# Making the chunk operators of an RWKV-7 recurrence for eight chunks at once

## The chip, the cores and the metric

The kernel runs on one core of one Trainium2 chip. The metric is the device time of one execution in microseconds (us). A difference of less than 0.3% is not told from no change.

## What is computed

One layer of a streaming encoder: 1024 prompt rows and 64 sample rows of width 1024 are normalised, multiplied by one input projection of 8320 columns, and split into differential attention (8 heads) and an RWKV-7 time mixing (16 heads of 64). Both results are gated and go through one output projection. The change touches the time mixing, whose definition is a scan over rows, for each head:

```python
def step(s, inp):                      # s: 64 x 64 state of a head
    r_t, w_t, k_t, v_t, a_t, b_t = inp
    sa = jnp.einsum('bhij,bhj->bhi', s, a_t)
    s = s * w_t[:, :, None, :] + sa[..., None] * b_t[:, :, None, :] + v_t[..., None] * k_t[:, :, None, :]
    return s, jnp.einsum('bhij,bhj->bhi', s, r_t)
```

The kernel does not walk row by row. It takes chunks of 64 rows. Within a chunk the rows' effects on each other form a 64 x 64 triangular system, which is inverted; between chunks only the state is carried.

## The kernel before

**Units.** The work of the time mixing is cut into 17 units: 8 pairs of heads, two halves of 512 rows each (8 chunks of 64), and one unit for the sample rows, in which each of the 8 "chunks" is one pair of heads. A tile holds head 0 of the pair in partitions 0 to 63 and head 1 in 64 to 127.

**Stages of a unit** (function `unit`, one generator for each unit):
- preparation (L536 to L677): up-projection of decay and learning rate with weights that `load_up` fetches (L514), cumulative decay, and the tiles `pt` (decayed rows) and `bk` (undecayed keys);
- products within the chunk (`m_s`, L689 and L690: 64 contraction rows, one head in each half of the array), masked by VectorE (L702) into `lt`, `pt` and `rbk`;
- the inverse of the triangular system (L719 to L829): five levels, each of two groups of small products, three VectorE operations between them, and one refinement; its result is `xtf`;
- transposes of `bk` and of the values, copied by ScalarE into `bkt` and `suv` (L789 to L815), once the unit before has left its chain;
- the chain over the 8 chunks (L860 to L913). `suv[:, c]` holds the state that chunk c starts from, beside the chunk's values. Each chunk takes three links: product `g` (L862), copied by VectorE (L876); product with the inverse (L879), copied back by VectorE into `suv` (L885, L886); product with `bkt` (L890), from which VectorE makes the next chunk's state (L900) with the decayed old state `sd` that ScalarE made (L869, L870). Two more products for each chunk give its outputs (L867 or L882, and L891);
- group norm, gate and store.

**What sets the order.** The program is written by a planner (`Weave`): each unit is a stream that yields the time it reckons its last step to take, and a filler stream of the lowest rank takes what is left of TensorE, three matmuls of an input projection at a time (L226 to L228). After the last head's projection the filler goes on with the output projection (L1236 to L1238). `turn` lets one unit at a time into each stage, so that one unit's chain lies beside the next one's inverse and the preparation of the one after. The order is fixed when the program is built; each engine then runs its own list in order and waits where an operand is late. Once all units are stored, attention (`phase_a`) takes the place of the units, with the same filler under it.

## Time and profile before

| what | value |
|---|---|
| median of 3 runs | 1816.07 us (1812.95 to 1818.63) |
| the profiled execution's own time | 1819.35 us |
| span of the profile | 1817.6 us |
| TensorE busy | 1678.9 us, 92% |
| VectorE busy | 1248.0 us, 69% |
| ScalarE busy | 846.4 us, 47% |
| GpSimd busy | 716.0 us, 39% |
| mean granted TensorE clock | 0.98 of full speed |

The profile is one execution. PE is TensorE, DVE is VectorE, ACT is ScalarE, POOL is GpSimd, SP is SyncE, whose queue issues most transfers. A busy TensorE need not be at its peak, since ends of matmuls overlap; what one costs is read from the distance between starts.

### The profile page before, as it was taken

To read this page: it belongs to the slowest core of one execution; us is meant where nothing else is said; L and a number is where in the kernel's file an instruction comes from. 1 tells how busy PE (TensorE), PEld (TensorE's weight loads), DVE (VectorE), ACT (ScalarE), POOL (GpSimd) and SP (SyncE) were. 2 spreads that over 40 slices of the span, in tenths; PEclk is the share of its full clock that TensorE was granted. 3 is DMA by queue.
4 is the path that set the end of the run, shared out by engine and by line. 5 is a ranking of instruction groups with operands and counts; after the bars stand their busy time and mean duration, and the time that the engine had idled before them with its cause. 6 is when DMAs were issued, how large, how long until landed. Compare 5 with 4: busy or idle time off the path is not lost.

```text
span 1817.6 us, 34309 instructions
## 1 busy us (share of the span) xinstructions
PE 1678.9 (92%) x12930; PEld 1500.6 (83%) x12930; DVE 1248.0 (69%) x2606; ACT 846.4 (47%) x2027; POOL 716.0 (39%) x901
## 2 busy tenths in 40 slices
PE   7999998999989989999999889989998898988997
PEld 5988888888878988898889888989887777777875
DVE  5667777678677778778777577744566476676736
ACT  6433443434433543444354344233556675665532
POOL 3433322332322433333342333112444757666563
PEclk9999999999999999999999899999999999999999
DMA  4210222221131111111111111436546455554345
GB/s 154 65 45 27 73 71 65 59 69 29 30 103 50 37 57 33 42 46 29 45 48 43 55 56 57 125 100 178 158 110 190 123 153 167 154 142 114 94 131 165
DMA packets 204096, 158.82 MB, mean 87 GB/s; under 512 B 44085, under 2 KB 185050, under 8 KB 203930
## 3 DMA queue, kind: packets, MB, share of 16 engines
q1 hardware_dynamic: 169098, 137.33, 26.3%
q10 hardware_dynamic: 34832, 19.30, 4.1%
q8 instruction: 102, 1.67, 0.4%
q14 instruction: 64, 0.52, 0.1%
HBM read 108.67 MB, written 47.34 MB: 86 GB/s over the span
## 4 chain that ended last, share of the span: by engine, by line
PE 56%; DVE 19%; POOL 7%; DMA 6%; issue 5%; ACT 5%; ACTq 1%; SPq 1%; POOLq 0%; DVEq 0%
PE x_o L1475 2%; PE po L1236 2%; PE po L1237 2%; PE po L1238 2%; PE cbank L890 2%; PE cbank L862 2%; PE s L1414 2%; PE m_s L689 2%; PE s L1415 1%; PE pj_g L226 1%; PE cbank L879 1%; PE pj_aq L226 1%; PE pj_av L226 1%; PE pj_g L227 1%; PE pj_k L226 1%
## 5 line engine op out<-in xcount | busy, mean ns | idle before, releaser
L869 ACT ACTIVATE sd<-suv,dc 64x64 f32<-64x64 f32 x128 | 44.4, 347 | 179.0 <-DVE suv L900 150.9
L1236 PE MATMUL po<-woh,mxh 128*128 128x512 f32 x288 | 122.1, 424 | 1.5 <-DVE part L1247 0.9
L1237 PE MATMUL po<-woh,mxl 128*128 128x512 f32 x288 | 115.7, 402 | 1.5 <-POOL mxl L158 1.5
L1238 PE MATMUL po<-wol,mxh 128*128 128x512 f32 x288 | 115.3, 400 | 1.8 <-POOL wol L158 1.8
L1431 ACT ACTIVATE e<-s,nb 128x128 f32<-128x128 f32 (+7 forms) x144 | 101.1, 708 | 33.5 <-DVE nb L1424 20.4
L158 POOL TENSOR_TENSOR mxl<-mxr,mxh 128x512 fp32r<-128x512 f32 x63 | 89.0, 1414 | 55.4 <-ACT mxh L157 53.0
L1475 PE MATMUL x_o<-vn,wt 128*128 128x128 f32 (+1 forms) x608 | 87.3, 289 | 11.8 <-DVE wt L1469 3.7
L1475 PEld LDWEIGHTS x_o<-vn,wt 128*128 128x128 f32 (+1 forms) x608 | 80.5, 200 | 21.0 <-DVE wt L1465 5.1
L1424 DVE TENSOR_REDUCE nb<-s 128x1 f32<-128x640 f32 (+8 forms) x104 | 95.5, 921 | 1.9
L735 POOL TENSOR_TENSOR ltlo<-lt,lt 64x512 f16<-64x512 f32 x32 | 37.6, 1173 | 129.4 <-ACT lt L723 128.2
L1414 PE MATMUL s<-k,qs 128*128 128x512 f32 (+4 forms) x208 | 76.6, 376 | 11.3 <-ACT e L1431 9.3
L900 DVE SCALAR_TENSOR_TENSOR suv<-cbank,dc,sd 64x64 f32<-64x64 f32 x224 | 63.1, 282 | 28.6 <-PE cbank L890 23.5
L890 PE MATMUL cbank<-suv,bkt 128*128 128x128 f32 x256 | 56.3, 302 | 24.5 <-DVE suv L886 24.3
L1415 PE MATMUL s<-k,qs 128*128 128x512 f32 (+4 forms) x208 | 71.2, 360 | 3.1 <-POOL k L1344 2.1
L226 PE MATMUL pj_k<-hhi,wh_k 128*128 128x384 f32 (+1 forms) x192 | 70.1, 365 | 1.9 <-ACT raw_k L241 1.9
L226 PE MATMUL pj_aq<-hhi,wh_aq 128*128 128x384 f32 (+1 forms) x192 | 71.5, 372 | 0.0
L226 PE MATMUL pj_av<-hhi,wh_av 128*128 128x384 f32 (+1 forms) x192 | 68.8, 358 | 2.5 <-DVE fl_g L999 2.1
L890 PEld LDWEIGHTS cbank<-suv,bkt 128*128 128x128 f32 x256 | 41.2, 189 | 36.0 <-DVE suv L886 33.9
L226 PE MATMUL pj_g<-hhi,wh_g 128*128 128x384 f32 (+1 forms) x192 | 70.6, 368 | 0.0
L226 PE MATMUL pj_ak<-hhi,wh_ak 128*128 128x384 f32 (+1 forms) x192 | 70.2, 365 | 0.0
L1247 DVE TENSOR_TENSOR part<-po,part 128x512 f32<-128x512 f32 x54 | 37.0, 686 | 47.7 <-PE po L1238 47.5
L226 PE MATMUL pj_v<-hhi,wh_v 128*128 128x384 f32 (+1 forms) x192 | 69.5, 362 | 0.0
(529 smaller groups left out, 6024.9 us busy)
## 6 DMA issues: line engine op xcount, KB each, us to landing
mxr<-mixB SPq DMA_DIRECT2D x32, 256.0 KB
wor<-in_w_out SPq DMA_DIRECT2D x64, 128.0 KB
qa<-scr_q SPq DMA_DIRECT2D x32, 204.0 KB
ka<-scr_k SPq DMA_DIRECT2D x32, 204.0 KB
mxr<-mixA SPq DMA_DIRECT2D x24, 256.0 KB
scr_q<-fl_q SPq DMA_DIRECT2D x8, 544.0 KB
scr_k<-fl_k SPq DMA_DIRECT2D x8, 544.0 KB
scr_v<-fl_v SPq DMA_DIRECT2D x8, 544.0 KB
```

The costliest lines, as they stand in the source:

```text
L158: gtt(lo, raw, hi.bitcast(F32), op=SUB)
L226: mm(ps[:, :n], hi[:, k, :], hhi[i][:, k, :], start=(k == 0), stop=False)
L890: mm(s, bkt[:, c], suv[:, c], start=True, stop=True)
L900: stt(suv[r, c + 1, h, :] if c < 7 and not smp else to[r], s[r, h * CH:(h + 1) * CH], dc[r, c:c + 1], sd[r], op0=MUL, op1=ADD)
L1236: mm(ps, hi[:, q, :], wh, start=(q == 0), stop=False)
L1237: mm(ps, lo[:, q, :], wh, start=False, stop=False)
L1238: mm(ps, hi[:, q, :], wl, start=False, stop=(q == len(ks) - 1))
L1414: mm(s2[:, b:b + w], lq, k1[c][:, k0 + o_:k0 + o_ + w], start=True, stop=False)
L1415: mm(s2[:, b:b + w], lq, k2[c][:, k0 + o_:k0 + o_ + w], start=False, stop=True)
L1424: nc.vector.tensor_reduce(nb[:, 0:m], s3[:, :, 0:n], axis=AX.X, op=MAX, negate=True)
L1431: act(e[:, 0:n], s3[:, j, 0:n], AF.Exp, bias=nb[:, j:j + 1], accum_out=st["sm"][:, c:c + 1])
L1475: mm(ops[:, 0:P], wt[0:w, b, :], vn[0:w, vb, :], start=(b == 0), stop=(b == len(kbs) - 1))
```

## The change

**The operators.** For each chunk the state map is now one 128 x 128 operator. The inverse is multiplied with the transposed decayed keys (`qt`, L861 of the changed kernel), the result with the transposed `bk` and the masked output products together (`ty`, L874), and VectorE adds that to an identity and to the decayed rows in place (L879). `pt` grows from 4 to 6 columns of 64 for it: two of raw products, two of state operator, two of output operator. `xtf` needs no zeros any more and is made by one operation instead of two. The masks take strict and inclusive part in one operation (4 in place of 6 for each half).

**The chain.** A chunk takes one product (L934); ScalarE scales it by the chunk's decay straight into the next chunk's `suv` (L943). The outputs of the chunk before are one product (L919), placed one step late.

**A second stream for each unit**, `side`, of a rank just under the unit's: it transposes `bk`, the decayed keys (`ptt`) and the values while the inverse runs, and copies them by ScalarE.

**The up-projection's weights** are issued by SyncE's queue instead of ScalarE's, and the sample unit's in 8 larger transfers instead of 32.

```diff
-                    nc.scalar.dma_start(out=t[r:r + 64, s, :], in_=I[nm][0, :, q * P:(q + 1) * P])
+                    nc.sync.dma_start(out=t[r:r + 64, s, :], in_=I[nm][0, :, q * P:(q + 1) * P])
...
-            yield lambda: turn["bk"] == n and all(("r", q) in have for q in need)
+            yield lambda: turn["bk"] == n and turn["chain"] >= n - 1 and all(("r", q) in have for q in need)
...
-                vtt(pt[r, :, 2 + h, :], c3(rm)[r], dd[r, :, 1:CH + 1], op=MUL)
+                vtt(pt[r, :, 4 + h, :], c3(rm)[r], dd[r, :, 1:CH + 1], op=MUL)
+                nc.scalar.copy(pt[r, :, 2 + h, :], bch(id64)[r])
...
+                for g in range(2):
+                    ps = yield from ps512(f"at{g}{u}")
+                    for i in range(4):
+                        nc.tensor.transpose(ps[:, i * P:(i + 1) * P],
+                                            pt[:, 4 * g + i, 0:2, :].rearrange("p s t -> p (s t)"), ident)
...
+                    nc.scalar.copy(ptt[:, 4 * g:4 * g + 4, :], ps.rearrange("p (c x) -> p c x", x=P))
...
-            for h in range(2):
-                r = slice(64 * h, 64 * h + 64)
-                vtt(xtf[r, :, h, :], c3(ps)[r], c3(xt)[r], op=ADD)
+            vtt(xtf, c3(ps), c3(xt), op=ADD)
...
+                        mm(ps[r, i * P:(i + 1) * P], xtf[r, 4 * g + i, :], ptt[r, 4 * g + i, :], start=True, stop=True)
+                nc.scalar.copy(qt[:, 4 * g:4 * g + 4, :], ps.rearrange("p (c x) -> p c x", x=P))
...
+                        mm(x[:, i * P:(i + 1) * P], qt[r, c, :], wb[r, c, 1:3, :], start=True, stop=True)
...
+                    vtt(o_, x.rearrange("p (c s t) -> p c s t", s=2, t=CH), o_, op=ADD)
...
             for c in range(8):
-                mm(g, pt[:, c, 0:2, :], suv[:, c], start=True, stop=True)
-                    mm(yc, pt[:, c, 2:4, :], suv[:, c], start=True, stop=False)
-                act(sd[0:64], suv[0:64, c, 0, :], AF.Copy, scale=dc[0:64, c:c + 1])
-                act(sd[64:128], suv[64:128, c, 1, :], AF.Copy, scale=dc[64:128, c:c + 1])
-                nc.vector.tensor_copy(gsb, g)
-                mm(uu, xtf[:, c], gsb, start=True, stop=True)
-                nc.vector.tensor_copy(suv[0:64, c, 0, :], uu[0:64, 0:CH])
-                nc.vector.tensor_copy(suv[64:128, c, 1, :], uu[64:128, CH:])
-                mm(s, bkt[:, c], suv[:, c], start=True, stop=True)
-                mm(yc, rbk[:, c], suv[:, c], start=False, stop=True)
+                mm(s, pt[:, c, 2:4, :], suv[:, c], start=True, stop=True)
...
-                    stt(suv[r, c + 1, h, :] if c < 7 and not smp else to[r], s[r, h * CH:(h + 1) * CH],
-                        dc[r, c:c + 1], sd[r], op0=MUL, op1=ADD)
+                    act(suv[r, c + 1, h, :] if c < 7 and not smp else to[r], s[r, h * CH:(h + 1) * CH],
+                        AF.Copy, scale=dc[r, c:c + 1])
+                if c:
+                    outputs(c - 1)
```

Below, `cbank` is the chain's PSUM bank, `y` its outputs' bank, `pj_` a projection of the filler. TensorE, in the first chunk of a chain (pair 3, first half), before:

```order
L862 MATMUL cbank<-suv_0_6633,pt_512 128x128
L867 MATMUL y_00_6693<-suv_0_6633,pt_512 128x128
L226 MATMUL pj_g_1_6864<-hhi_170,wh_g_6528 128x384
L227 MATMUL pj_g_1_6864<-hlo_173,wh_g_6528 128x384
L228 MATMUL pj_g_1_6864<-hhi_170,wl_g_6529 128x384
L226 MATMUL pj_g_1_6864<-hhi_170,wh_g_6528 128x384
L227 MATMUL pj_g_1_6864<-hlo_173,wh_g_6528 128x384
L228 MATMUL pj_g_1_6864<-hhi_170,wl_g_6529 128x384
L879 MATMUL cbank<-gsb_03_6911,xtf 128x128
```

And in the same unit's chain now:

```order
L934 MATMUL cbank<-suv_0_6071,pt_512 128x128
L226 MATMUL pj_g_2_6536<-hhi_171,wh_g_6053 128x320
L227 MATMUL pj_g_2_6536<-hlo_174,wh_g_6053 128x320
L228 MATMUL pj_g_2_6536<-hhi_171,wl_g_6054 128x320
L919 MATMUL y_00_6553<-suv_0_6071,pt_512 128x128
L226 MATMUL pj_g_2_6536<-hhi_171,wh_g_6053 128x320
L227 MATMUL pj_g_2_6536<-hlo_174,wh_g_6053 128x320
L228 MATMUL pj_g_2_6536<-hhi_171,wl_g_6054 128x320
L934 MATMUL cbank<-suv_0_6071,pt_512 128x128
```

Before, six projection matmuls stood between the first and the second of three links of a chunk; now three, an output product and three more stand between one chunk's only link and the next chunk's.

TensorE, between the end of a unit's inverse (`m_iz`) and the first product of its chain, before:

```order
L823 MATMUL m_iz_00_8333<-xt_0_8174,q_r_0_8260 64x64
L965 MATMUL m_zt_10_8352<-ident,ycp 128x128 x4
L226 MATMUL pj_k_1_8298<-hhi_170,wh_k_7873 128x384
L227 MATMUL pj_k_1_8298<-hlo_173,wh_k_7873 128x384
L228 MATMUL pj_k_1_8298<-hhi_170,wl_k_7874 128x384
L862 MATMUL cbank<-suv_0_8292,pt_512 128x128
```

At this place now stand, each twice for a unit, a group of eight `m_qt` and a group of eight `m_ty` (the end of the second `m_qt` group and the first `m_ty` group):

```order
L861 MATMUL m_qt_00_8096<-ptt_0_7537,xtf 64x128 x8
L226 MATMUL pj_g_0_8034<-hhi_169,wh_g_7735 128x384
L227 MATMUL pj_g_0_8034<-hlo_172,wh_g_7735 128x384
L228 MATMUL pj_g_0_8034<-hhi_169,wl_g_7736 128x384
...
L874 MATMUL m_ty_00_8118<-wb_0_7416,qt_0_8082 128x128
L874 MATMUL m_ty_01_8119<-wb_0_7416,qt_0_8082 128x128
L874 MATMUL m_ty_00_8118<-wb_0_7416,qt_0_8082 128x128
L874 MATMUL m_ty_01_8119<-wb_0_7416,qt_0_8082 128x128
```

The inverse used to be followed by the chain directly; now the operators' products stand between them.

ScalarE, at the end of a chain, before (`raw_` and `mr` are the filler's, `t_wup` the up-projection's weights):

```order
L241 COPY raw_r_7060<-pj_r_0_7062 128x384
L519 DMA t_wup_7659<-in_w_up 64x128 x2
L519 DMA t_wup_7659<-in_a_up 64x128 x2
L869 ACTIVATE sd_07_7263<-suv_0_6633,dc_0_5492 64x64
L870 ACTIVATE sd_07_7263<-suv_0_6633,dc_0_5492 64x64
L241 COPY raw_r_7060<-pj_r_1_7180 128x384
```

And along a whole chain now:

```order
L241 COPY raw_v_7270<-pj_v_0_7272 128x384
L943 ACTIVATE suv_1_6798<-cbank,dc_1_6215 64x64 x2
L561 CAST t_wus_1_7727<-t_wup_7399 128x256
L577 ACTIVATE t_sq_1_7762<-mk_1_6959,pv 128x512
L943 ACTIVATE suv_1_6798<-cbank,dc_1_6215 64x64 x6
L241 COPY raw_v_7270<-pj_v_1_7323 128x384
L394 ACTIVATE mv_0_7483<-raw_v_7270,omu 128x512
L943 ACTIVATE suv_1_6798<-cbank,dc_1_6215 64x64 x2
L924 COPY ysb_1_7322<-y_10_7348 64x256
L926 COPY ysb_1_7322<-y_10_7348 64x256
L943 ACTIVATE suv_1_6798<-cbank,dc_1_6215 64x64 x4
L943 ACTIVATE st_1_7445<-cbank,dc_1_6215 64x64 x2
```

The transfers have left ScalarE's list, and the chain's link runs through it, behind evacuations and copies of other streams.

## Rows read from the trace of the kernel before

**Rows 1.** The page: busy time, share and instructions of each engine.
```profile
PE 1678.9 (92%) x12930; PEld 1500.6 (83%) x12930; DVE 1248.0 (69%) x2606; ACT 846.4 (47%) x2027; POOL 716.0 (39%) x901
```

**Rows 2.** Stretches: length, PE, PEld, DVE, ACT, POOL busy; clock; DMA share; GB/s.
```profile
60.00:1250.00 1190.00, 1123.10 (x9770) 1027.33 (x9770) 865.60 (x1906) 493.15 (x1116) 374.08 (x445) 0.99 0.20 57
1250.00:1818.00 568.00, 511.19 (x2913) 433.79 (x2911) 348.16 (x637) 316.17 (x842) 319.70 (x405) 0.96 0.52 146
```

**Rows 3.** PE's waits, 60 to 1250 us: total us, times, longest.
```profile
PE cbank L890 <- DVE suv L886: 24.3, 24, 3.7
PE m_ip L742 <- DVE x L761: 7.3, 8, 2.5
PE m_iq L752 <- DVE q L746: 7.0, 7, 3.2
PE cbank L862 <- DVE suv L900: 5.3, 5, 2.5
PE cbank L879 <- DVE gsb L876: 4.4, 7, 1.8
```

**Rows 4.** Timeline of PE at two chain products: start us, length us, what.
```profile
619.48 0.38 PE L862 MATMUL cbank<-suv,pt 128*128 128x128 f32 x2
619.70 0.39 PE L867 MATMUL y<-suv,pt 128*128 128x128 f32 x2
619.84 0.42 PE L226 MATMUL pj_ag<-hhi,wh_ag 128*128 128x384 f32 x1
620.10 0.34 PE L227 MATMUL pj_ag<-hlo,wh_ag 128*128 128x384 f32 x1
620.28 0.34 PE L228 MATMUL pj_ag<-hhi,wl_ag 128*128 128x384 f32 x1
```

**Rows 5.** The same timeline, at a group of half-array products.
```profile
621.50 0.38 PE L879 MATMUL cbank<-gsb,xtf 128*128 128x128 f32 x2
621.81 0.37 PE L689 MATMUL m_s<-pt,bk 64*128 64x128 f32 x1
...
622.70 0.27 PE L690 MATMUL m_s<-pt,bk 64*128 64x128 f32 x1
622.90 0.44 PE L226 MATMUL pj_ag<-hhi,wh_ag 128*128 128x384 f32 x1
623.18 0.34 PE L227 MATMUL pj_ag<-hlo,wh_ag 128*128 128x384 f32 x1
```

**Rows 6.** Timeline of PE at a group of four transposes.
```profile
508.24 0.60 PE L618 MATMUL m_ib<-ident,t_inx 128*128 128x128 f32 x4
508.60 0.42 PE L226 MATMUL pj_av<-hhi,wh_av 128*128 128x384 f32 x1
508.86 0.33 PE L227 MATMUL pj_av<-hlo,wh_av 128*128 128x384 f32 x1
```

**Rows 7.** Timeline of DVE at the copy behind Rows 5's L879.
```profile
621.92 0.22 DVE L885 COPY suv<-cbank 64x64 f32<-64x64 f32 x1 [1.40 <-PE cbank L879]
```

**Rows 8.** Timeline of ACT at a chunk's two scalings of the state.
```profile
618.12 0.35 ACT L869 ACTIVATE sd<-suv,dc 64x64 f32<-64x64 f32 x1 [3.45 <-DVE suv L900]
618.49 0.34 ACT L870 ACTIVATE sd<-suv,dc 64x64 f32<-64x64 f32 x1
```

**Rows 9.** Groups of DVE and ACT: busy us, mean ns; idle before, releaser.
```profile
L900 DVE SCALAR_TENSOR_TENSOR suv<-cbank,dc,sd 64x64 f32<-64x64 f32 x224 | 63.1, 282 | 28.6 <-PE cbank L890 23.5
L876 DVE COPY gsb<-cbank 128x128 f32<-128x128 f32 x128 | 36.5, 285 | 29.5 <-PE cbank L862 27.9
L828 DVE TENSOR_TENSOR xtf<-m_iz,xt 64x512 f32<-64x512 f32 x32 | 22.0, 686 | 0.3
L798 ACT COPY bkt<-m_kt 128x512 f32<-128x512 f32 x32 | 18.7, 585 | 32.9 <-PE m_kt L795 32.6
```

**Rows 10.** Issues of the up-projection's weights: ns min/median/max, first and last start.
```profile
L519 ACTq DMA_DIRECT2D t_wup<-in_w_up x48: 472/552/1417, 1.3 to 1055.5; - x48
L519 ACTq DMA_DIRECT2D t_wup<-in_a_up x48: 472/608/1455, 2.5 to 1061.8; - x48
```

More of the change, by code (lines that the diff above doesn't have):

```diff
@@ L510, in next_up @@
         def next_up(n):
-            if n < len(order) and order[n][0] is not None:
-                nxt.append(load_up(order[n][0]))
+            if n < len(order):
+                nxt.append(load_up4(0, 0) if order[n][0] is None else load_up(order[n][0]))
         def load_up(q):
@@ L704, in unit @@
-            soon.add(("v", p, hf))
-            yield lambda: all(("v", q) in have for q in need)
-            if not smp:
-                vw = mt_["v", p, hf]
-            pb = yield from ps512(f"bo{u}")
-            mm(pb, bdr, kbh, start=True, stop=False)
-            mm(pb, bdr, kbl, start=False, stop=True)
-            spend(450)
-            yield LAT
-            yield lambda: turn["norm"] >= n - 1
-            bv = t512("bv", 2, nm=u)
-            vtt(bv, pb, vw[:, 64:576], op=MUL)
-            done(op_(DVE, 512))
@@ L717, in unit @@
-            turn["prep"] = n + 1
+                e4, o4 = (x.rearrange("p (c s t) -> p c s t", s=2, t=CH) for x in (pe, po))
+                lo_r, hi_r = slice(0, 64), slice(64, 128)
+                for i, (o_, s_, r) in enumerate((
+                        (wb[lo_r, gs, 0::2, :], e4, lo_r), (wb[hi_r, gs, 0::2, :], o4, hi_r),
+                        (pt[hi_r, gs, 0::4, :], e4, hi_r), (pt[lo_r, gs, 1::4, :], o4, lo_r))):
+                    vtt(o_, s_[r], msk[r].unsqueeze(1).to_broadcast([64, 4, 2, CH]), op=MUL)
+                    yield near(DVE, 512) if i < 3 else done(op_(DVE, 512), 2)
@@ L719, in unit @@
+            weave.add(n + 0.5, side())
             xt = t512("xt", 2, F16, nm=f"a{u}")
@@ L903, in unit @@
+                    ybank.append(psy.tile([P, HALF], F32, tag="y", name=f"y{u}{c}"))
+                y = ybank[-1]
+                mm(y[:, (c % 4) * P:(c % 4 + 1) * P], pt[:, c, 4:6, :], suv[:, c], start=True, stop=True)
+                spend(230)
                 if c % 4 == 3:
```

257 lines of the change are left out of this document (143 added, 114 removed).

## The prediction

> **What bounds the kernel now.** First the page: PE is busy 1678.9 of 1817.6 us, no other engine more than 69% [rows 1]. Then the windows, cut where the time mixing ends: from 60 to 1250 us, the units' part, PE is busy 1123.1 of 1190.0 us, 94%, with DVE at 73% and ACT at 41%; in the attention part after it PE is at 90% [rows 2]. So I took TensorE's own list as what sets the end in both parts. The reason is the filler: every gap in a unit gets projection matmuls, and what is not done under the units is done under attention. A unit that gets through faster leaves more filler to the attention part; it doesn't by itself shorten anything. The first score product stands before 288 rows of projections in the old order and before 504 in the new, three projections of 72 rows more. The end moves by two things only: what PE's list costs, and how long PE stands still in it.
>
> The standstills are in the list of waits. The chain's three links held PE for 24.3, 5.3 and 4.4 us, together 34; the inverse's two products, which wait for VectorE, 7.3 and 7.0 us [rows 3]. All are waits for DVE.
>
> The cost of a product I read from the timeline, as the delay that it causes in the row of projections around it. A projection matmul follows the one before by 0.18 us (620.10 to 620.28). From L862's start at 619.48 to the start of the second projection after, 620.10, is 0.62; less one 0.18 leaves 0.45 for two products, 0.224 each [rows 4]. For a group of eight half-array products (four chunks, two heads): from L879 at 621.50 to the second projection after, 623.18, is 1.68; less L879's 0.224 and 0.18 leaves 1.28 [rows 5]. Of these, the heads' products run side by side: 16 records, two for each product, start between 621.81 and 622.70, so a pair of products takes 0.22 and four of them 0.87, and 0.41 of the 1.28 lies at the two ends of the group. Four transposes: 508.24 to 508.86 less 0.18 is 0.44, so 0.11 each [rows 6].
>
> **The change part by part.**
>
> *A, PE's list.* A chunk had five products of 0.224 us and has two. With 8 chunks and 17 units, 3 x 136 x 0.224 = 91 us go. For each unit come eight transposes of the decayed keys, 8 x 0.11 = 0.88, and four groups of eight half-array products, two `qt` and two `ty`. `ty` has just the shape of the group in [rows 5]; `qt` has 64 output columns as well as 64 contraction rows, and no f32 product of that shape stands in the trace; I take the same 1.28, as the nearest row. That is 0.88 + 5.12 = 6.0 for a unit, 102 us in all. A is **+11 us**: PE gets more work, not less. Ends: if `qt`'s two heads don't run side by side, its group costs four times 0.22 more, 2.16; 2 x 17 x 0.88 is 30 more, +41. If the 0.41 at the ends of the new groups vanished, 4 x 17 x 0.41 is 28 less, -17.
>
> One rule of the skill bears on this. The row shows a group at 1.28 where its pairs alone take 0.87. The Trainium skill (TensorE: Matmul & The Clock Gate, "Measured speedup vs the span model") gives a packed group the span of one matmul and about 4 ns for each further tile; by that four pairs would cost no more than their 0.87, and A would be the -17 above. The row has the ends of the group in it, so I go by the row.
>
> *B, the chain's waits.* The 34 us of the three links go with them. A new link takes their place, `suv` from ACT to the next L934, 136 times. How long it takes: a product's start to the copy behind it 0.42 (621.50 to 621.92) [rows 5, 7]; ACT's two scalings 0.37 apart and 0.34 long, 0.71 [rows 8]; so 1.13 and a hand-over back to PE. What covers it in the new order: the product, two triples of projections and the output product, 0.22 + 6 x 0.18 + 0.22 = 1.5 us, less where the projections are 320 wide. So it fits, by 0.2 to 0.4, as long as ACT is free. ACT is at 41% there [rows 2] and gets more: for each unit four copies of `bk` for two, two of `ptt`, two of `qt`, two of the identity, eight more of about 0.585 [rows 9], or 80 us in all, 48%. The cover of an old link was about as large: L862 behind two scalings on DVE waited 5.3 us, 0.04 a link; L890 behind two copies waited 24.3, 0.18 a link, with DVE at 73%. I take the middle, 0.12: 136 x 0.12 = 16 us. Ends: 5; and 40, if half of the links find a copy of 0.585 before them in ACT's list. Behind such a wait stand the whole of PE's list, so it costs in full. B is **-34 + 16 = -18 us**.
>
> *C, VectorE's relief.* Of the groups shown, the state's update (63.1 us), the copy of `g` (36.5) and half of `xtf` (11) leave DVE, and the copies back to `suv` besides; four additions for a unit come, 68 x 0.686 = 47 us [rows 9]. DVE's 865.6 us [rows 2] fall to 802, from 73% to 67%, and lower with those copies. The inverse's steps now find it free more often: of the 14.3 us of waits in L742 and L752 I take half, **-7 us** (0 to -14).
>
> *D, work I cost at nothing.* ACT's own load: hidden by PE's list except in the link of B. The masks keep their data in fewer, larger operations. The identity and `bk` copies are made under the projections while the inverse, which is longer, runs; if `qt` found `ptt` late, the unit would wait and the filler would run, at no cost to PE. After `ty` the additions on DVE (two of 0.69 behind the last group) have 2.6 us of projections before the first L934; without that cover 17 x 1.7 = 29 us would show. The wait for `turn["chain"]` holds back one unit's `pt` until the chain two before it is over, which its buffer wanted anyway. The weights' issues: 96 of about 0.58 us leave ACT's list, 56 us [rows 10], which is where the scalings of the old chain stood behind them; on SyncE they queue behind stores of the filler. They are issued at the same place as before, a unit's stage ahead of their use, and that stage hides the queue; were it longer, the cast L561 would block ACT and with it the chain. The sample unit's four steps of loading lie under the filler as its two did.
>
> *Sum:* 11 - 18 - 7 = -14 us on the profiled execution's 1819.35, or 1805. That execution is 3.3 above the median, so **1802 us** for the median.
>
> **The rivals.**
>
> *The link through ACT is the new bound* (slower). L934 waits for ACT's list: evacuations of the filler (L241) and copies wait there for PE and DVE themselves, and the scalings stand behind them. Place: PE at L934, released by ACT. Price: against the sum above, each 0.1 us a link is 14 us; from 0.22 a link on the kernel is no faster than before; at 0.35 a link the time is 1802 + 31 = 1833. For it: cover exceeds need by 0.2 to 0.4 only, and eight copies a unit are added on that engine. Against it: DVE, busier than ACT will be, cost the old state link 0.04. The Trainium skill (ScalarE: Activation LUTs, "Rules for kernel authors") advises VectorE over ScalarE for multiplications and budgets about 0.3 us and 0.83 ns an element for an ACTIVATE; by that, an estimate of 0.35 for 64 elements, the measured 0.34 agrees, and DVE's 0.282 for the same step [rows 9] would leave the link 0.15 more room.
>
> *`qt`'s quarters don't run side by side* (slower): A is +41, time 1832. Against it: the half-array groups do [rows 5].
>
> *Nothing to see*: the chain's waits move to the new link in the same size (0.25 a link), or VectorE's relief shows nowhere because the waits of the inverse are its own latency; time 1811 to 1821, say 1816. For it: PE's list is as long as before.
>
> *Clearly faster*: the group's ends overlap with the projections (A at -17), or the new link waits as little as the old state link (5 for 16) and the inverse's waits go (-14 for -7); 1802 less 28 or 18, about 1778. For it: the old state link's row.
>
> **How the numbers follow.** The forecast, with its own range of 1788 to 1810, has 0.42; clearly faster 0.17; nothing to see 0.16; the link through ACT 0.15; the quarters 0.10. A difference under 0.3%, 5.4 us, is no change. Faster is then 0.59, same 0.16, slower 0.25. The range of 1768 to 1834 takes in the middle of each rival and leaves out the ends of A (-17 with all else good) and of the link (over 0.35).
>
> **What would show it.** In the profile after: a group of eight `qt` or `ty` costs PE about 1.28 us (A); `cbank` is released by ACT and waits some 16 us in all, with nothing left of waits for L876 to L900 (B); DVE at 67% or less and L799 and L808, the inverse's products, wait under 10 us (C); a chain of eight chunks takes 8 x 1.5 = 12 us, and the end moves little for it; three more projections stand under attention; SyncE's weights are there before the cast. Wrong would be: PE's busy time well under 1679, or a wait of more than 0.2 us a link, or PE waiting for `up`.

## Result, and the profile after

The changed kernel takes **1863.21 us** (median of 4 runs, 1860.33 to 1869.17) against 1816.43 beside it: a ratio of 1.0264, 95% interval 1.023 to 1.0297. It is slower by 2.6%; 1802 was forecast, with a range to 1834. The profiled execution took 1860.42 us, its span is 1858.6.

The page, in the form of [rows 1]:

```profile
PE 1690.4 (91%) x13338; PEld 1491.6 (80%) x13338; DVE 1142.7 (61%) x1909; ACT 913.2 (49%) x2159; POOL 701.9 (38%) x891
```

PE is busy 11.5 us longer, VectorE 105 us shorter. Neither shows where 41 us went. The windows do, cut at the first score product (1273.5 us before, 1278.4 after), in the columns of [rows 2]:

```profile
60.00:1278.00 1218.00, 1123.03 (x10093) 1003.52 (x10091) 757.45 (x1192) 557.31 (x1241) 366.36 (x438) 0.98 0.19 54
1278.00:1859.00 581.00, 522.84 (x2998) 448.54 (x2998) 352.16 (x653) 317.37 (x846) 315.05 (x407) 0.95 0.51 145
```

The units' part is about as long as before, but less filler was done in it. The same windows for the filler's line L226 alone, one in three of its matmuls, to the end of the last chain and from the first score product on, before:

```profile
0.00:1229.30 1229.30, 505.81 (x1386) 263.41 (x1386) 0.99 0.21 60
1273.50:1818.00 544.50, 33.22 (x96) 18.27 (x96) 0.96 0.50 141
```

and after:

```profile
0.00:1237.20 1237.20, 493.49 (x1326) 255.68 (x1326) 0.98 0.19 56
1278.40:1859.00 580.60, 59.50 (x168) 32.59 (x168) 0.95 0.51 145
```

So all kernels below are compared by a **net price**: the length of a part less 0.166 us for each projection matmul in it. (That is the distance between the starts of two that follow each other at full clock, in either kernel: median 0.176 for 384 columns, 0.147 for 320, two of the first to one of the second.) The units' part, to the first product of the last chain's last chunk, costs 1229.3 - 3 x 1386 x 0.166 = 539 us net before and 1237.2 - 3978 x 0.166 = 577 after. The attention part, from the first score product, costs 544.1 - 288 x 0.166 = 496 before and 580.2 - 504 x 0.166 = 496.5 after. So 38 of the 41 us are lost in the units' part; the other 3 lie between it and the first score product.

What is it there? PE's waits of 60 to 1278 us, in the columns of [rows 3]:

```profile
PE cbank L934 <- ACT suv L943: 30.5, 15, 4.5
PE m_ip L799 <- DVE x L818: 11.2, 15, 1.6
PE m_qt L861 <- DVE xtf L851: 10.3, 10, 2.2
PE m_iz L848 <- DVE q_r L842: 10.1, 9, 1.6
PE m_zt L1002 <- DVE ycp L971: 6.3, 6, 2.8
PE m_iq L809 <- DVE q L803: 5.4, 5, 1.6
PE m_ip L799 <- DVE x_a L789: 3.6, 3, 2.9
PE cbank L934 <- DVE pt L879: 2.9, 3, 1.2
```

The chain waits 34 us, as before, 31 of them now for ScalarE; the steps of the inverse and the product behind it wait 44 (20 before). The whole list adds up to 87 us, before to 66. And the clock: up to the first score product 13 stretches of together 61.5 us were granted half of full speed, 1.2 instead of 2.4 GHz; before, 5 of 24 us.

**An account of the whole.** Three terms make up a span: what PE's list takes by itself, the time that PE stands still (all idle times of 0.15 us and more before a matmul), and half of the half-clock time outside these standstills, since half of its work would have been done anyway. Standstills are 126.2 us before and 154.6 now, half-clock time outside them 66.5 and 94.0. What is left for the list is 1817.6 - 126.2 - 33.3 = 1658 before and 1858.6 - 154.6 - 47.0 = 1657 now. So the new operators' list costs what the old one did; of the 41 us, 28 are standstills and 14 the clock. For the units' part alone the same sum gives +22 for standstills, +13.5 for the clock and +2 for the list.

One of the standstills, on ScalarE's timeline (at the end of a line the idle time before it, and what ended it):

```profile
732.36 0.34 ACT L394 ACTIVATE rs__502<-raw_r,omu 128x64 f32<-128x64 f32 x1
740.75 0.72 ACT L682 ACTIVATE t_kbh<-t_kb,dv 128x512 fp32r<-128x512 f32 x1 [8.05 <-DVE t_kb L671]
741.38 0.46 ACT L241 COPY raw_v<-pj_v 128x384 f32<-128x384 f32 x1
741.74 0.40 ACT L561 CAST t_wus<-t_wup 128x256 fp32r<-128x256 f32 x1
742.61 0.72 ACT L577 ACTIVATE t_sq<-mk,pv 128x512 f32<-128x512 f32 x1 [0.47 <-DVE t_kbl L683]
743.24 0.61 ACT L943 ACTIVATE suv<-cbank,dc 64x64 f32<-64x64 f32 x2
```

on VectorE's:

```profile
731.15 2.48 DVE L660 TENSOR_TENSOR pt<-t_kkn,dd 64x512 f32<-64x512 f32 x2
733.66 1.68 DVE L664 SCALAR_TENSOR_TENSOR t_th<-t_th,t_kkn 128x512 f32<-128x512 f32 x1
735.26 1.28 DVE L879 TENSOR_TENSOR pt<-m_ty,pt 128x512 f32<-128x512 f32 x2
736.46 1.82 DVE L401 SCALAR_TENSOR_TENSOR mr<-raw_r,pv,mr 128x512 f32<-128x512 f32 x1
...
739.24 0.69 DVE L668 TENSOR_TENSOR bk<-t_kb,t_cs 64x512 f32<-64x512 f32 x1
740.03 0.69 DVE L671 TENSOR_TENSOR t_kb<-t_kb,mr 128x512 f32<-128x512 f32 x1
```

and on PE's:

```profile
738.58 0.38 PE L934 MATMUL cbank<-suv,pt 128*128 128x128 f32 x2
...
743.91 0.80 PE L934 MATMUL cbank<-suv,pt 128*128 128x128 f32 x2 [3.88 <-ACT suv L943]
744.36 0.67 PE L226 MATMUL pj_v<-hhi,wh_v 128*128 128x384 f32 x1
744.82 0.52 PE L227 MATMUL pj_v<-hlo,wh_v 128*128 128x384 f32 x1
745.14 0.52 PE L228 MATMUL pj_v<-hhi,wl_v 128*128 128x384 f32 x1
```

Read them from PE backwards. The chain's first product stands at 738.58, its scaling L943 starts at 743.24, since ScalarE stood for 8.05 us before L682, a copy of the next unit's preparation, and L943 stands behind that in its list. L682 waited for VectorE's L671, and VectorE had been busy without a gap since 730. PE stood 3.88 us with one product and 1.1 us of filler in hand, and right there, at 742.5, a half-clock stretch of 6.8 us begins: the next two projections start 0.46 and 0.32 after the one before; behind the product at 738.58 it was 0.27 and 0.17. Gaps of 1.85 us and more stand in seven chains, 27.5 us of the 34 in all, six of the seven in second halves. ScalarE's wait for L671 is the largest of its list; for the same copy it was 14.6 us before:

```profile
ACT t_kbh L682 <- DVE t_kb L671: 85.2, 16, 8.7
```

### The profile page after: what moved, and what is told of

Its sections match the earlier page's. It is cut to its first block, busy times and chain, and to the rows that moved or that the text cites. A ratio compares the mean times of both kernels' runs of the same rounds, so it can differ in the third digit from the quotient of the medians.

```text
span 1858.6 us, 34603 instructions
## 1 busy us (share of the span) xinstructions
PE 1690.4 (91%) x13338; PEld 1491.6 (80%) x13338; DVE 1142.7 (61%) x1909; ACT 913.2 (49%) x2159; POOL 701.9 (38%) x891
## 5 line engine op out<-in xcount | busy, mean ns | idle before, releaser
L158 POOL TENSOR_TENSOR mxl<-mxr,mxh 128x512 fp32r<-128x512 f32 x63 | 84.6, 1345 | 61.5 <-ACT mxh L157 55.0
L943 ACT ACTIVATE suv<-cbank,dc 64x64 f32<-64x64 f32 x224 | 69.0, 308 | 71.1 <-PE cbank L934 65.5
L934 PE MATMUL cbank<-suv,pt 128*128 128x128 f32 x256 | 60.3, 319 | 34.2 <-ACT suv L943 30.5
L803 DVE TENSOR_TENSOR q<-m_ip,mt 128x512 f16<-128x512 f32 x80 | 54.9, 687 | 47.5 <-PE m_ip L799 47.2
L934 PEld LDWEIGHTS cbank<-suv,pt 128*128 128x128 f32 x256 | 44.3, 202 | 48.7 <-ACT suv L943 41.3
L226 PE MATMUL pj_v<-hhi,wh_v 128*128 128x384 f32 (+1 forms) x192 | 77.1, 401 | 0.0
L792 POOL TENSOR_TENSOR ltlo<-wb,lt 64x512 f16<-64x512 f32 x32 | 40.3, 1258 | 93.4 <-ACT lt L780 92.3
L226 PE MATMUL pj_k<-hhi,wh_k 128*128 128x384 f32 (+1 forms) x192 | 71.8, 374 | 1.8 <-ACT raw_k L241 1.8
L1273 PEld LDWEIGHTS po<-woh,mxh 128*128 128x128 f32 x288 | 55.5, 193 | 20.8 <-ACT woh L157 9.9
L226 PE MATMUL pj_aq<-hhi,wh_aq 128*128 128x384 f32 (+1 forms) x192 | 71.7, 373 | 0.0
L226 PE MATMUL pj_g<-hhi,wh_g 128*128 128x384 f32 (+1 forms) x192 | 71.4, 372 | 0.0
L226 PE MATMUL pj_av<-hhi,wh_av 128*128 128x384 f32 (+1 forms) x192 | 69.2, 360 | 0.0
```

The costliest lines, as they stand in the source:

```text
L158: gtt(lo, raw, hi.bitcast(F32), op=SUB)
L226: mm(ps[:, :n], hi[:, k, :], hhi[i][:, k, :], start=(k == 0), stop=False)
L934: mm(s, pt[:, c, 2:4, :], suv[:, c], start=True, stop=True)
L943: act(suv[r, c + 1, h, :] if c < 7 and not smp else to[r], s[r, h * CH:(h + 1) * CH], AF.Copy, scale=dc[r, c:c + 1])
L1273: mm(ps, hi[:, q, :], wh, start=(q == 0), stop=False)
```

## Experiments

All of them in one table first. "Unit" is the net time from one unit's chain end to the next, over units 0 to 11; "units" and "attention" are the net parts defined above, in the one profiled execution of each; "left" is the projection matmuls that still stood behind the first score product. "Stood" and "half" are PE's standstills and the half-clock time outside them over the whole span, and "list" is the span less "stood" and half of "half". Runs with one letter stand against runs of the kernel before on the same chip, whose medians were 1816 to 1821 us. Executions of one kernel differ by up to 10 us from the median, and the parts come from one execution each; that of e2 was its shortest, 1804.96.

| kernel | median us | ratio to before, 95% | unit | units | attention | left | stood | half | list |
|---|---|---|---|---|---|---|---|---|---|
| before | 1816.4 | | 29.0 | 539 | 496 | 288 | 126 | 67 | 1658 |
| after | 1863.2 | 1.023 to 1.030 | 31.3 | 577 | 496 | 504 | 155 | 94 | 1657 |
| e1 copy on VectorE | 1856.0 | 1.019 to 1.024 | 30.1 | 566 | 500 | 504 | 151 | 84 | 1658 |
| e2 before, queue part only | 1815.2 | 0.997 to 1.000 | 29.0 | 525 | 496 | 312 | 125 | 38 | 1659 |
| e3 scaling on VectorE | 1856.5 | 1.018 to 1.025 | 30.9 | 565 | 498 | 504 | 154 | 80 | 1655 |
| e4 four copies off ScalarE | 1868.7 | 1.025 to 1.031 | 31.7 | 581 | 500 | 504 | 160 | 98 | 1658 |
| f1 rule in all chains | 1900.1 | 1.042 to 1.048 | 30.4 | (575) | 510 | 0 | 195 | 88 | 1656 |
| f2 and preparation after chain | 1959.5 | 1.074 to 1.081 | 31.3 | (636) | 510 | 0 | 230 | 139 | 1656 |
| f3 constant 1.35 | 1892.0 | 1.037 to 1.043 | 29.7 | (548) | 527 | 0 | 179 | 96 | 1659 |
| f4 before, constant 1.35 | 1935.3 | 1.060 to 1.067 | 29.5 | (593) | 528 | 0 | 193 | 155 | 1663 |
| g1 constant 1.15 | 1844.8 | 1.011 to 1.016 | 31.1 | 572 | 494 | 168 | 143 | 98 | 1654 |
| g2 pause 3 us | 1854.2 | 1.017 to 1.022 | 30.2 | 555 | 514 | 504 | 147 | 95 | 1659 |
| g3 pause 3 us, copy | 1846.5 | 1.012 to 1.018 | 30.0 | 552 | 516 | 504 | 142 | 103 | 1658 |
| g4 `ty` twice | 1888.9 | 1.036 to 1.041 | 32.6 | 601 | 500 | 504 | 154 | 88 | 1688 |
| h1 rule in second halves | 1867.6 | 1.027 to 1.031 | 30.6 | 559 | 526 | 0 | 155 | 107 | 1657 |
| h2 pause, copy, 1.15 | 1823.9 | 1.003 to 1.006 | 29.2 | 540 | 507 | 96 | 130 | 85 | 1654 |
| h3 pause 3.6 us | 1864.1 | 1.026 to 1.031 | 31.4 | 570 | 508 | 504 | 155 | 92 | 1660 |
| h4 before, pause 3 us | 1849.7 | 1.018 to 1.023 | 31.3 | 577 | 491 | 360 | 144 | 94 | 1657 |
| i1 before, constant 1.15 | 1848.9 | 1.013 to 1.020 | 28.3 | 537 | 524 | 0 | 142 | 94 | 1656 |
| i2 pause, copy, 1.2 | 1856.3 | 1.018 to 1.024 | 30.0 | 554 | 526 | 0 | 144 | 137 | 1649 |

In brackets: the filler ended before the last chain did, so the part holds idle time for want of filler. Read the last column first: but for g4, whose list was made longer, it is 1649 to 1663 us in all of these programs, old and new. So what sets them apart is how long PE stands still and how long it runs at half clock.

### The link and its engine: e1 to e4

e1 moves L682, e3 the link itself to VectorE, e4 the copies of `ptt` and `qt`; e2 is the kernel before with nothing of the change but the weights' queue.

```diff
e1:
-                act(kbh, kb, AF.Copy, scale=hrk[:, p:p + 1])
+                vts(kbh, kb, hrk[:, p:p + 1], None, op0=MUL)
e3 (L943):
-                    act(suv[r, c + 1, h, :] if c < 7 and not smp else to[r], s[r, h * CH:(h + 1) * CH],
-                        AF.Copy, scale=dc[r, c:c + 1])
+                    vts(suv[r, c + 1, h, :] if c < 7 and not smp else to[r], s[r, h * CH:(h + 1) * CH],
+                        dc[r, c:c + 1], None, op0=MUL)
e4 (L739; L864 likewise):
-                    nc.scalar.copy(ptt[:, 4 * g:4 * g + 4, :], ps.rearrange("p (c x) -> p c x", x=P))
+                    nc.vector.tensor_copy(ptt[:, 4 * g:4 * g + 4, :], ps.rearrange("p (c x) -> p c x", x=P))
```

> One instruction of each head unit moves from ScalarE to VectorE: the scaled copy t_kbh (L682 of the changed kernel), which in ScalarE's list stands ahead of a chain's scalings and idles there up to 8.7 us for VectorE. Theory 1 (ScalarE's list is blocked by that one copy): TensorE's waits at L934 for ScalarE fall from 30.5 us to under 12, the half clock in the units' part from some 54 us to under 40, and the time from 1863 to 1823 to 1843. Theory 2 (ScalarE simply has too much to do): it loses 0.72 us of work a unit, 12 us of 913, so the waits stay above 25 and the time within 5 us of 1863. Theory 3 (TensorE's own list is what costs): within 5 us of 1863.

> The kernel before with one part of the change alone: the up-projection's weights issued by SyncE's queue, the sample unit's in larger pieces. All theories that put the loss into the chain or TensorE's list: within 5 us of 1816. If the loss comes from weights that SyncE issues late, it appears here: 1840 or more, with TensorE or ScalarE released by the transfer t_wup.

> The chain's scaling (L943) by VectorE instead of ScalarE, in the same order of TensorE's list. Theory 1, extended (the unit's preparation is late on VectorE, and whatever stands behind it in an in-order list is late too): the scalings now stand in VectorE's own list behind the late preparation, so TensorE still waits 20 us or more at L934, released by VectorE, and the time is 1850 to 1870. Theory 2 (ScalarE is the wrong engine for the link): waits under 12 us and 1825 to 1840.

> The copies of ptt and qt (four of about 0.6 us a unit, 40 us in all) go from ScalarE to VectorE; the copy t_kbh stays on ScalarE. Theory 1 (one blocked instruction): TensorE's waits at L934 stay at 25 to 35 us and the time within 12 us of 1863. Theory 2 (ScalarE's load): the waits fall under 15 us and the time to 1845 or less.

e2 costs nothing: the loss does not come from the queue. e4 took 4 copies a unit off ScalarE and was no faster, and the wait at L934 was 34.4 us: ScalarE's load is not the cause. e1 and e3 are each some 7 us shorter, with intervals that touch the changed kernel's. In e1 the wait at L934 is hardly less (under 12 was expected, and 1823 to 1843 for the time), and in e3 it only changes its engine:

```profile
PE cbank L934 <- ACT suv L943: 25.2, 15, 3.8
```

```profile
PE cbank L934 <- DVE suv L943: 32.9, 14, 5.0
```

(e1 first, then e3.) In e1, with L682 gone from ScalarE's list, the next thing in it does the same; its timeline:

```profile
462.83 0.41 ACT L561 CAST t_wus<-t_wup 128x256 fp32r<-128x256 f32 x1 [4.17 <-DVE bk L666]
463.14 0.62 ACT L943 ACTIVATE suv<-cbank,dc 64x64 f32<-64x64 f32 x2
```

L561 is the cast of the unit after next, which waits for VectorE to be done with a buffer. So it is not one copy: whatever stands ahead of the link and waits for VectorE's late list holds it, on either engine.

### Later units kept out of the chain, and a slower planner: f1 to f4

f1 gives the planner a rule: while a chain is emitted, streams of later units rest. f2 adds that a unit's decayed keys wait for the chain before it. f3 and f4 (the latter on the kernel before) reckon each evacuation 1.35 times as long.

```diff
f1, in Weave.run:
+                if self.hold < s[0] < 50:
+                    continue
...
             yield lambda: "suv" in made and turn["chain"] == n
+            weave.hold = n
...
             yield outputs(7)
+            weave.hold = 99
f2:
-            yield lambda: turn["bk"] == n and turn["chain"] >= n - 1 and all(("r", q) in have for q in need)
+            yield lambda: turn["bk"] == n and turn["chain"] >= n and all(("r", q) in have for q in need)
f3, f4:
-RS = 1.0
+RS = 1.35
```

> The changed kernel with one rule added to the planner: while a unit's chain of eight products is being emitted, no step of a later unit is emitted, only filler and the steps of earlier units. Nothing is left out. Theory 1 (the standstills at L934 come from steps of the next units, late on VectorE, that stand in the in-order lists ahead of the chain's scalings): the waits at L934 fall from 30.5 to 12 us or less, the 4 us standstills go, the half-clock time falls from 118 us to 95 or less, and the time to 1825 to 1840. Rival (the link is too short by itself, whatever stands around it): the waits at L934 stay at 25 us or more and the time within 6 us of 1861. A third case: the late steps were emitted before the chain began, so that the rule comes too late for them; then the standstills stay, at the chain's first two products.

> As the run with the rule, and besides the next unit's preparation (the decayed keys, L653 to L683) waits until the chain of the unit before it is over, where the changed kernel lets it start one unit earlier. Nothing is left out. Theory 1: VectorE has no preparation in hand either when the additions behind ty run, so the waits at L934 fall below 8 us, and the inverse's waits (L799, L842, L848, L851, L861: 44 us) stay, since another unit's preparation now falls under the inverse; time 1815 to 1835. Rival (the link alone): as the changed kernel, 1855 to 1867. If the time rises above 1867, PE has run out of other work in the places where the preparation used to be.

> The changed kernel with the planner's cost of every VectorE, ScalarE and GpSimd operation 1.35 times as long (one constant, 1.0 to 1.35), so that more filler is put between a product and the one that waits for its evacuation. Nothing is left out. Theory 1 in a wide form (the planner's costs are too short for engines that fall behind in the dense order): both the chain's waits and the inverse's fall, together from 78 to 50 us or less, and the time to 1825 to 1845. Rival: PE's standstills are one long lateness at each unit's end, several us long, which 0.2 us more of filler at each step does not cover: waits 65 us or more and time 1850 or more.

> The kernel before with the same constant at 1.35: the control of the run above. If the planner's costs hit only the new order, the time stays within 8 us of 1817; if they hit both, it falls by as much as the changed kernel's does, and the change's loss of 45 us stays as it is.

The waits at L934 for ScalarE fell: to 11.7 us in f1 as expected, to 9.8 in f2 (below 8 was expected), to 10.4 in f3. A unit's price in f1 and f3 went from 31.3 to 30.4 and 29.7. But the inverse and the product behind it waited longer, 76, 87 and 59 us in place of 44 (part of it after the filler's end), so that f3's two sorts of wait together stayed where its rival put them. And the times missed in all four: each is slower than its own base, f4 too, for which neither case had a rise. Much of that is the filler. A unit of f1 takes 75 us instead of 67 and holds 270 projection matmuls instead of 214, so all 4680 are used up before the last chain. From its end to the first score product PE then stands still for 29 of 33 us, and attention, with nothing to fill it, costs 510 to 528 instead of 496. A time of a whole kernel therefore has two halves: a unit's price, and whether filler is left at the end.

### A milder planner, a pause, and PE's list by itself: g1 to g4

```diff
g1:
-RS = 1.0
+RS = 1.15
g2, before the chain's first product (g3: with e1's line too):
-            yield LAT
+            yield 3000
             ybank = []
g4:
+                for _ in range(2):
                     for i in range(4):
...
                                 mm(x[:, i * P:(i + 1) * P], qt[r, c, :], wb[r, c, 1:3, :], start=True, stop=True)
-                spend(1100)
+                spend(2200)
```

> The changed kernel with the planner's constant at 1.15. Nothing is left out. Counted is the net time of a unit: the time from one unit's chain end to the next unit's, less 0.166 us for each projection matmul that stands in it; over the units 0 to 11 that is 29.0 us before, 31.3 in the changed kernel, 29.7 with the constant at 1.35 (which ran out of filler before the last units). Theory 1 (lateness in dense lists, which more filler at each step covers): net 30.1 to 30.8, filler left for attention, and so the gain shows in the end: 1836 to 1852. Rival (the unit pace alone decides, slower units are slower kernels): 1866 or more.

> The changed kernel with one pause in the planner: 3 us between the last addition behind ty and the first product of the chain, which fills with some 18 projection matmuls for each unit. No engine's work changes; nothing is left out. Theory 1 (the chain's standstills are one lateness of up to 4.5 us at its start): the waits at L934 fall from 30.5 to 10 us or less, the half-clock stretches that began there go, the net time of a unit falls from 31.3 to 29.8 to 30.3, and the end to 1835 to 1848. Rival (each link short by itself): waits at L934 at 22 us or more, time 1855 to 1868.

> The same pause, and the copy kbh (L682) on VectorE as in the run with that edit alone (1855.95). Theory 1: the two act on one lateness, so they add less than fully: waits at L934 at 6 us or less, net time 29.6 to 30.1, end 1830 to 1844. Rival: no better than the copy alone, 1850 to 1860.

> The changed kernel with each ty product made twice in the same place (the planner is told so), 34 groups of eight more: the price of PE's list by itself. If a group costs 1.28 us and costs it in full, the net time of a unit rises by 2.56 to 33.9 and the end by 44, to 1900 to 1910. If the cost of added PE work is partly hidden by PE's standstills of 87 us, less: 1865 to 1890. If the standstills grow with it, more than 1915.

g4 is the price of PE's list. The time rises by 25.7 us by the medians, but PE's standstills and clock moved as well; the list itself is 31 us longer, 0.91 for each of the 34 groups. The timeline says the same. One of the doubled groups, and the second projection behind it:

```profile
272.73 2.06 PE L875 MATMUL m_ty<-wb,qt 64*128 64x128 f32 x32
275.00 0.33 PE L227 MATMUL pj_g<-hlo,wh_g 128*128 128x384 f32 x1
```

275.00 - 272.73 - 0.18 is 2.09, the median of 32 such groups too; a single group in the changed kernel takes 1.19 (below). So the second costs 0.90: less than the 1.28 forecast for one, and near the four pairs alone, 0.87 by [rows 5], since two groups back to back pay the ends once. PE's work counts in full.

g2 and g3 gave the units 22 and 25 us back, but not in the way that was expected. The waits at L934 were to fall to 10 and 6 us (g2 and g3; the rival of g2 had 22 or more):

```profile
PE cbank L934 <- ACT suv L943: 23.6, 22, 4.9
```

```profile
PE cbank L934 <- ACT suv L943: 16.0, 17, 3.9
```

So a pause ahead of the chain does not clear its standstills; the waits at L934 fell by 7 and 14.5 us, and the rest of the gain came in other places. Only 9 and 17 us of it reached the end: attention cost 514 and 516. Attention's instructions stand in another order there (of 2998 on PE, 938 have the same line at the same place in g2 as in the changed kernel), and 72 us of it ran at half clock instead of 54.5. g1 gained 18 us, but hardly by what was expected: a unit costs 31.1, above the 30.1 to 30.8 forecast; fewer projections are left for attention, and PE stood 12 us less over the whole.

### What sets the order, and the controls: h1 to h4, i1, i2

```diff
h1:
-            weave.hold = n
+            weave.hold = n if hf == 1 else 99
h4, in the kernel before:
-            yield LAT
+            yield 3000

             for c in range(8):
                 g = ps128()
```

h2 is g3 with `RS = 1.15`, i2 with 1.2; h3 is g2 with 3600; i1 is the kernel before with 1.15.

> The changed kernel with the rule of f1 (no step of a later unit while a chain is emitted) in the chains of second halves only. Nothing is left out. Theory 1: the standstills at L934 began in these chains, so the waits there fall from 30.5 to 12 us or less; the pace stays fast enough that filler is left at the last chain; the units' part costs 555 to 565 us net of filler (576.9 in the changed kernel) and the end is 1838 to 1852. Rival (the steps of later units in first-half chains matter as much): waits at L934 above 20 us and net above 570.

> The pause of 3 us, the copy kbh on VectorE and the planner's constant at 1.15 together. Nothing is left out. Theory 1: waits at L934 below 12 us, the units' part 545 to 552 net of filler, which is the kernel before plus the 11 us of more PE work, within 5 us; if the attention part returns to 494 to 500, the end is 1822 to 1834, still not below 1816. Rival (the pause itself harms the attention part): attention 512 or more, end 1840 or more.

> The changed kernel with a pause of 3.6 us in place of 3. If the attention part's 514 us with 3 us came of the order that the planner happened to give, this one is another draw: 494 to 508 there, units 550 to 560 net of filler, end 1836 to 1848. If the pause itself harms it, 512 or more and 1852 to 1860.

> The kernel before with the same pause of 3 us ahead of its chain: the control. Theory 1: its chain of three links has no late steps in front of it to cover, so the units' part stays within 5 us of 539 net of filler, and the time within 10 us of 1818, the attention part's order being redrawn. Rival (any order gains by a pause there, so the new chain is nothing special): net 525 or less.

> The kernel before with the planner's constant at 1.15: nothing else differs. Theory 2 (the order that the planner draws decides, the kernel before is a good draw): its units' part rises from 539 to 548 or more net of filler, and the time to 1826 or more. Rival (the old code is robust, and h4 was an exception, because its chain now waits behind the pause three times a chunk): 533 to 545 net, 1808 to 1824.

> The changed kernel with the 3 us pause, the copy kbh on VectorE and the planner's constant at 1.2. Theory 2: another draw; units' part 538 to 556 net, attention 494 to 516, end 1810 to 1845, and no draw of the new code below 1805, since its PE list is longer than the old one. Rival (the constant is what helps, the more the better, until filler runs out): units 539 or less and 1825 or less.

**In h1 the waits did not fall, and its trace shows why.** The wait at L934 (here L938) is 36 us, in the very chains that the rule should clear. Its ScalarE timeline:

```profile
488.12 0.63 ACT L947 ACTIVATE suv<-cbank,dc 64x64 f32<-64x64 f32 x2 [0.65 <-PE cbank L938]
488.78 0.48 ACT L244 COPY raw_v<-pj_v 128x384 f32<-128x384 f32 x1
494.68 0.72 ACT L685 ACTIVATE t_kbh<-t_kb,dv 128x512 fp32r<-128x512 f32 x1 [5.42 <-DVE t_kb L674]
495.31 0.62 ACT L947 ACTIVATE suv<-cbank,dc 64x64 f32<-64x64 f32 x2
```

The next unit's copy (L682, here L685) stands in the middle of the chain, where the rule forbids it. In ScalarE's list of that program, at another such chain (the last number of a name counts on in the order in which the planner writes; only L685 and L947 are shown):

```
186 L685 ACTIVATE t_kbh_0_2593<-t_kb_0_2308,dv 128x512
188 L947 ACTIVATE suv_1_1912<-cbank,dc_1_1374 64x64 x2
191 L947 ACTIVATE suv_1_1912<-cbank,dc_1_1374 64x64 x6
...
198 L947 ACTIVATE st_1_2461<-cbank,dc_1_1374 64x64 x2
```

The planner wrote the copy after the chain's last state (2593 after 2461), and it stands before the chain's first scaling. The planner's order is not the engine's: a later step of the build orders each list once more and takes forward what depends on nothing in the chain. In the changed kernel it is the same: `t_kbh_0_2449` was written between the sixth and the seventh product of its chain and stands before the first scaling. Eight links that depend on each other are overtaken by whatever doesn't; when that is late, the links are. This also qualifies f1 and the pauses: they change what the planner writes, and only by way of the later step what each engine runs.

**The controls.** The same pause of 3 us makes the kernel *before* 2% slower (h4), its units' part as dear as the change's, 577. PE's waits in its units' part add up to 87 us and 65 us of it ran at half clock, as after the change (87 and 61.5), but in other places; the three links of its chain hold PE for 28 us, and what grew is this:

```profile
PE m_zt L965 <- DVE ycp L934: 20.5, 12, 3.0
PE m_ip L742 <- DVE x L761: 14.5, 15, 2.6
```

And the changed kernel in the order of h2 has 67 us of waits, 41 at half clock, and a units' part of 540, the same as before, with all of the new products in it. (The waits at L934 are still 19.1 us in h2, where under 12 was expected.) So a loss of this size does not need the new chain, and the new chain does not need to have it. The other draws missed too: a pause longer by 0.6 us (h3) gives back 7 us of the units' part in place of 22, where 17 to 27 was expected; h4's two cases, 539 and 525 or less, had no 577; i1 keeps the units' part at 537, as its rival said, but is 1.6% slower, as its theory said, because it ran out of filler and attention cost 524. What is the change's and what is its order's, by the draws that still had filler at the last chain: old code 525 (e2), 537, 539 and, with the pause, 577; new code 540 to 581 in eleven (g4 aside), 563 in the mean, against 545 for the four. With four old draws, one execution each, that does not settle whether the new code is worse in a typical order; it shows that the order alone moves either by some 40 us. h2 is the best of the new code, still 0.3 to 0.6% slower than before; i2, one step further, cost 554 in the units, ran out of filler and lost it again (1810 to 1845 was expected). No version beat the kernel before by more than can be measured.

## Why the prediction was wrong

The sum was -14 us; the profiled executions differ by +41. In the units' part, term by term: A was +2 (+11 forecast), B 0 (-18), C +24 (-7), and the clock, for which there was no term, +13.5; other waits fell by 2 to 3. The steps that failed are C, B and the missing clock, in this order of size.

**A, PE's list (+11): a size, too large.** A group of the new products on PE's timeline, between projections:

```profile
399.17 1.16 PE L874 MATMUL m_ty<-wb,qt 64*128 64x128 f32 x16
400.26 0.44 PE L226 MATMUL pj_g<-hhi,wh_g 128*128 128x384 f32 x1
400.54 0.34 PE L227 MATMUL pj_g<-hlo,wh_g 128*128 128x384 f32 x1
```

Read as in [rows 5], 400.54 - 399.17 - 0.18 is 1.19; the `qt` groups come to 1.12, so its quarters do run side by side and that rival is out. With these A is 17 x (0.88 + 2 x 1.12 + 2 x 1.19) - 91 = +2.5 us, and the account of the units' part gives +2. The 1.28 came from a group with a chain product in front of it; where the same kind of group stands between projections, it took 1.19 in the kernel before as well (14 groups). By the Trainium skill (TensorE: Matmul & The Clock Gate, "Measured speedup vs the span model"), which gives a packed group the span of one matmul and about 4 ns for each further tile, a group would cost no more than its pairs. The trace does not agree for a group that stands alone among projections, which still pays its ends, 1.12 to 1.19 against 0.87; for the second of two back to back, in g4, it does, 0.90.

**B, the chain's waits (-34 + 16): 18 us too low.** The 34 us of the old links went; the new chain waited 34, 30.5 of it for ScalarE's link (16 forecast) and 2.9 in its first product for the additions behind `ty`, which D had at nothing. The term was a small shortfall at each of 136 links, 0.12 us, the middle of two old links' means. Most links wait for nothing: 15 waits hold the 30.5 us, up to 4.5 each, and the long ones stand behind another unit's late work in ScalarE's list. The sum's upper end priced that list as "a copy of 0.585 before them", by the length of what stands ahead and not by what it waits for itself. The rival of the link through ACT did say that copies there wait themselves, and named the right engine and place; it was priced by means all the same, and with the measured mean of 0.22 a link it would have given about 1816. The prediction's own sign of being wrong, a wait of more than 0.2 us a link, was met.

**C, VectorE's relief (-7): the wrong sign, and the largest miss.** VectorE fell to 757 of 1218 us, 62%, below the 67% forecast, and the inverse with the product behind it waited 44 us instead of 20. The two products that C counted wait 20 (L799, L809) for 14 before; `m_iz` 12.6, where it waited for nothing before; and `qt` 10.3, for the inverse's last step. For a `qt` that finds an operand late (it named `ptt`) D had said that "the filler would run, at no cost to PE"; PE stood there, because the order is fixed. Those waits follow when VectorE is late, not how much it has to do: it stood idle at other times, and in the stretch above had 12 us without a gap. What makes it late has the form of B again, on VectorE's list. There another unit's preparation stands ahead of the inverse's step and itself waits for GpSimd, or takes longer than usual (last section):

```profile
723.15 0.43 DVE L604 COPY t_inx<-inv 128x512 f32<-128x512 f32 x1 [1.76 <-POOL inv L601]
723.50 0.69 DVE L842 TENSOR_TENSOR q_r<-m_ir,qt 128x512 f16<-128x512 f32 x1
```

```profile
724.24 0.44 PE L848 MATMUL m_iz<-xt,q_r 64*64 64x64 f16 x16 [1.07 <-DVE q_r L842]
```

That is read from the traces; no run moved these operations, so how much of the 24 us it explains stays open.

**The clock, not in the sum.** Each of the six standstills of 3.9 us and more at L934 has a half-clock stretch that starts in it or within 0.3 us of its end; up to the first score product there are 61.5 us of it instead of 24. The sum priced a standstill at its own length only. Standstills +22, the clock +13.5 and A's +2 make up the 38 us that the units' part lost.

**D, nothing:** held for the queue (e2) and ScalarE's load (e4), not for `qt` and the additions (above). Its sentence on `L561`, that a late cast "would block ACT and with it the chain", is what e1 shows, with VectorE as the cause instead of a transfer.

**The filler:** that three projections move under attention was right (504 for 288), read from the programs, and attention cost the same net. What shows only in the experiments is the other end: with none left, attention costs 510 to 528.

What stays open is why VectorE is late where it is: whether the new operators bring that about in any order, or the one order that the planner and the build gave them.

## What to carry to other kernels

Where a chain of dependent links goes through an engine's in-order list, read in that list what stands ahead of each link and what *that* waits for; the mean wait of the old link says nothing about it. Split a span into PE's list, its standstills and its half-clock time before looking for a cause: here the list was the same to 1 us. Before blaming an edit in a program whose order a planner makes, nudge the planner in the old kernel too (a pause, a constant): here a pause alone cost 2%, where the edit cost 2.6%. And count work that moves between parts out of both, or a part that was handed filler looks slower than it is.

## What was not expected of the hardware

A standstill costs more than its length. The granted clock around the one shown above, in the columns of [rows 2]:

```profile
736.00:739.90 3.90, 3.90 (x23) 3.71 (x23) 3.87 (x6) 0.00 (x0) 1.78 (x3) 1.00 0.23 67
743.00:749.20 6.20, 5.29 (x20) 5.29 (x21) 0.00 (x0) 2.77 (x9) 0.16 (x1) 0.50 0.00 0
```

PE was busy without a gap until 739.9, stood 3.88 us, and got 0.50 of the clock for the 6.2 us after.

And VectorE's operations of one shape did not take one time. Two operations of the preparation, now:

```profile
L660 DVE TENSOR_TENSOR pt<-t_kkn,dd 64x512 f32<-64x512 f32 x32 | 35.6, 1112 | 0.4
L664 DVE SCALAR_TENSOR_TENSOR t_th<-t_th,t_kkn 128x512 f32<-128x512 f32 x16 | 27.6, 1723 | 0.5
```

and the same two before:

```profile
L651 DVE TENSOR_TENSOR pt<-t_kkn,dd 64x512 f32<-64x512 f32 x32 | 27.1, 847 | 0.5
L655 DVE SCALAR_TENSOR_TENSOR t_th<-t_th,t_kkn 128x512 f32<-128x512 f32 x16 | 12.0, 749 | 0.3
```

1112 against 847 ns and 1723 against 749, 24 us in all. Sorted by what GpSimd does at the time, the records of the changed kernel fall apart. L668, which stands there too, took 689 ns in the mean of the 8 times that GpSimd was idle for nine tenths of it or more, and 1798 in the 4 that GpSimd was busy for nine tenths or more; L666 681 (11 times) and 1464 (4). Under none of L664's 16 was GpSimd idle. The masks (L708), which read one operand from PSUM, took 684 to 688 ns either way. So here GpSimd's work goes with slow VectorE operations where both operands lie in SBUF. No run moved GpSimd's work to try it, but in the stretch from 731.0 to 738.3 us, where the slow ones stand, GpSimd was busy 6.71 of 7.3 us and VectorE 7.26: it is part of why VectorE's list is late just there.
